# GpSimd's additions given to VectorE, one layer's constants made earlier, and another order of the last outputs: a two-layer hybrid transformer kernel

## The chip, the cores and the metric

The kernel runs on one core of one Trainium2 chip. The metric is the device time of one execution in microseconds (us). A core has five engines that run side by side and wait for one another by semaphores: TensorE (PE in the profile, with its weight loads as PEld), VectorE (DVE), ScalarE (ACT), GpSimd (POOL) and SyncE (SP), which issues the transfers between HBM and the on-chip memory SBUF. TensorE writes its products to PSUM, which is divided into banks of 128x512 floats. Each engine works through its own instructions in the order in which they stand in the program: an instruction that waits holds up everything behind it on its engine.

## The reference, cut to what matters

Two layers of a diffusion backbone over 1024 latent tokens and 256 context tokens, model width 1024, all in float32:

```python
for l in range(2):
    h  = rms_norm(x, g1[l]) * (1 + sc1) + sh1          # sh, sc, gt: silu(c) @ w_mod[l] + b_mod[l]
    mix = concat(window_attention(rope(q), rope(k), v), # 8 heads on 2 KV heads, +-128 tokens and the context
                 fourier_mix(u, w_fourier[l]),          # 2-D DFT per group of channels, then a linear map
                 gla(gq, gk, gv, gr, gz))               # gated linear attention in chunks of 64, both directions
    x  = x + gt1 * (mix @ w_out[l])
    h2 = rms_norm(x, g2[l]) * (1 + sc2) + sh2
    gate, up = split(h2 @ w_ffn_in[l])                  # 1024 -> 2 x 2816
    x  = x + gt2 * ((silu(gate) * up) @ w_ffn_out[l])   # 2816 -> 1024
    # layer 0 does the same for the context tokens
```

## The kernel before, in words

Activations lie with features on the 128 partitions: a feature block of 128 by 512 tokens is one tile, and the 1024 latent tokens are two halves, c = 0 and c = 1. A float32 product is made of three passes (`mm3`, lines 168 to 170): each operand is split by `split` into a rounded high part (a cast on ACT, line 163) and the rest, value minus high part (a subtraction on DVE, line 164), and TensorE adds high times high, high times rest and rest times high. So each weight tile and each activation tile costs one ACT cast and one DVE subtraction before TensorE can use it. In the profile `wh`, `wl` and `HC` are split weights, `F`, `H` and `HC` split activations, `raw` and `XC` weights as loaded, and `f`, `mm`, `t`, `g` PSUM banks (four `f`, two of each other).

A layer has a mixed stage (projections, attention, Fourier mixing, gated linear attention, output projection, woven together), then the FFN, then the down projection. Layer 0 runs to about 1705 us of the trace, layer 1 from there to the end.

- **The mixed stage.** `project` makes queries and keys with their rotary factors (line 597 the multiplication by the sine, on POOL). `attend` and `gla` run beside it; in `gla` line 876 adds two masked 128x256 halves and line 906 multiplies the normalised output by a gate tile `sr` that has just been loaded, both on POOL. `layer_consts(l)` at the start of each layer loads the gate weights, the Fourier weights and constants of that layer, and makes `a12` from them by eight small matmuls (line 229; two rows of four in the order).
- **The FFN.** `ffn_plain` does the first few of the 22 blocks f of 128 hidden channels in the usual way. `ffn_seven` does the rest, both token halves at once, with seven products in place of eight for a two-by-two block product (gate and up against feature halves; the Winograd form of Strassen's scheme). For that it needs sums of activations, made once (`combos1` and `combos2`, lines 1156 and 1164: the differences and the running sum on POOL, the sums with "+" in their names on DVE), and for each f five sums of 128x512 weight tiles (`weights`, line 1222, on POOL, tile `c`), each then split by ACT and DVE. Weights are made three products ahead of their use. The four results of an f are put together by ACT copies and DVE additions (lines 1268 to 1286), and the last read of a PSUM bank frees it for a later product. In layer 0 the modulation vectors of layer 1 are made on the side: two 128x1024 tiles of `wmodT` for each f are loaded into `raw` and reduced on DVE (line 328).
- **The down projection** (`ffn_lat`, `down_mm`). For each half c it goes over all 22 f, and for each f over the 8 output blocks m, adding into 8 PSUM banks: m = 0 to 3 are `f` banks, 4 and 5 are `mm`, 6 and 7 are `t`. `done(m)` (line 1370) adds the finished block to the residual on DVE, which frees its bank, and stores it. After c = 1 of layer 0 comes layer 1: `layer_consts(1)`, and the first projection of its mixed stage (lines 516 to 518: high by high, high by rest, and `wl` by high).

What sets the order: the program emits work as interleaved streams with planned costs, and a scheduler of the Tile framework places each instruction in its engine's order. TensorE has 12,699 rows in that order; in the mixed stages about a thousand of them stand elsewhere after the change.

Of the kernel before, what the change touches and what calls it, by code (L numbers as in the profile page):

```python
# [16 lines left out]
KT = 8  # L17
# [3 lines left out]
FT = 22  # L21
# [3 lines left out]
FS = ("F", 20)  # L25
LAG = 3
REST = (32, 20)
NA = 6
# [16 lines left out]
class Prog:  # L45
# [374 lines left out]
    def layer(self, l):  # L420
        nc, tc = self.nc, self.tc
        need = l < DEPTH - 1
        self.layer_consts(l)
        XA = self.XA = self.t(self.bp, [128, 8, 512], F32, "XA", 1)
# [160 lines left out]
    def qk(self, l, s, nm, j, ps, t0, n, rope):  # L585
# [9 lines left out]
        if rope is not None:  # L595
            nc.vector.stream_shuffle(sq, raw, mask=[(i + 16) % 32 for i in range(32)])
            nc.gpsimd.tensor_tensor(sq, sq, rope[:, 1, :], ALU.mult)
            nc.vector.tensor_tensor(raw, raw, rope[:, 0, :], ALU.mult)
            nc.vector.tensor_tensor(raw, raw, sq, ALU.add)
# [122 lines left out]
    def gla(self, l, s, need):  # L722
# [34 lines left out]
        for j in range(2):  # L757
# [99 lines left out]
            for c in range(nq):  # L857
# [3 lines left out]
                for hh in range(2):  # L861
                    qd, en, st, _ = heads[hh]
                    tps = []
                    for d in range(2):
                        tp = self.g_ps(cw)
                        rows = slice(d * 64, d * 64 + 64)
                        for b in range(cw // 128):
                            bs = slice(c * cw + b * 128, c * cw + (b + 1) * 128)
                            nc.tensor.matmul(tp[:, b * 128:(b + 1) * 128], en[rows, bs], qd[rows, bs], start=True, stop=True)
                        tps.append(tp)  # L870
                    at = tmp("e")
                    for z in range(0, cw, 256):
                        for d in range(2):
                            nc.vector.copy_predicated(
                                self.abuf[d], self.glam[d][:].rearrange("p a b -> p (a b)"), tps[d][:, z:z + 256])
                        nc.gpsimd.tensor_tensor(at[:, z:z + 256], self.abuf[0], self.abuf[1], ALU.add)
                    ats.append(at)
                    yield 2.0
# [26 lines left out]
                nc.sync.dma_start(sr, self.dram[s, "sr"][j, :, cs])  # L905
                nc.gpsimd.tensor_tensor(ob, ob, sr, ALU.mult)
                nc.sync.dma_start(self.dram[s, "mix"][:, 6 + j, cs], ob)
# [243 lines left out]
    def combo(self, name, pool, tag, parts):  # L1151
        self.B[name] = self.half(pool, tag)
        for k in range(4):
            a, b, op = parts(k)
            t = self.t(self.tp, [128, 512], F32, "nx", 3)[:]
            (self.nc.vector if "+" in name else self.nc.gpsimd).tensor_tensor(t, a, b, op)
            self.split(t, *self.B[name](k))
            yield 1

    def combos2(self):  # L1160
        r, x = self.raw0, self.raw1
        yield from self.combo("7+", self.fp, FS, lambda k: (r(k + 4), x(k + 4), ALU.add))
        for k in range(4):
            self.nc.gpsimd.tensor_tensor(r(k), r(k), x(k), ALU.add)
            yield 1
# [33 lines left out]
    def ffn_seven(self, l, fs, fps):  # L1199
# [7 lines left out]
        def weights(i):  # L1207
# [12 lines left out]
            if isinstance(pair, tuple):  # L1220
                src = self.t(self.tp, [128, 512], F32, "c1", 2)[:]
                nc.gpsimd.tensor_tensor(src, *pair)  # L1222
            else:
# [73 lines left out]

    def down_mm(self, ps, w, g, f, ms):
        for m in ms:
            s = slice(m * 128, (m + 1) * 128)  # L1300
            self.mm3(ps[m], w[0][:, s], w[1][:, s], g[:, 0, :], g[:, 1, :], f == 0, f == FT - 1)

    def ffn_lat(self, l):
# [5 lines left out]
        with tc.tile_pool(name=f"ffn{l}", bufs=2, reuse_waits="tile") as self.fp, \  # L1309
# [13 lines left out]
            for f in self.ffn_seven(l, list(range(f0, FT)), fps):  # L1323
                if mod is not None:
                    if f == f0 + 4:
                        nrc = self.t(self.tp, [128, NC], F32, "nrc", 1)
                        nc.vector.tensor_copy(nrc[:], self.norm_stats(self.streamed(self.xcsrc, 0, NC), NC, True))
                    for _ in range(2):
                        next(mod, None)
# [12 lines left out]
            for c in range(2):  # L1342
# [33 lines left out]
                else:  # L1376
                    for m in range(KT):
                        done(m)
# [111 lines left out]
```

## Time and profile before

| | |
|---|---|
| three runs, median (lowest to highest) | 3032.04 us (3027.81 to 3037.07) |
| the profiled execution: its own time / span of the trace | 3032.16 us / 3030.4 us |
| mean granted TensorE clock over the span | 0.959 of full speed |
| PE busy | 2810.1 us (93%) |
| DVE busy | 1925.5 us (64%) |
| ACT busy | 1362.1 us (45%) |
| POOL busy | 365.6 us (12%) |

The span runs from the first to the last record of the trace; about 1.8 us of the execution lie outside it. An engine's busy time counts its instructions' own duration, not its waits. The granted clock of TensorE has two levels, 1.2 and 2.4 GHz, written as 0.5 and 1.0.

### The profile page before, as it was taken

What the parts mean: (1) busy time and instruction counts of PE and PEld (TensorE: products, weight loads), DVE (VectorE), ACT (ScalarE), POOL (GpSimd) and SP (SyncE); (2) the same over time, 40 slices, a digit from 0 to 9 for tenths busy, and PEclk for the clock granted to TensorE, in tenths of its full rate; (3) what the DMA queues carried; (4) which work ended last, traced back from release to release, by engine and by line L of the source; (5) the groups of instructions that cost most, each with busy time, mean ns of one, the idle gap of its engine ahead of it and who ended that gap; (6) DMA issues with size and microseconds to landing.
All of it is one profiled execution on the core that took longest, in us unless ns stands there. A gap on an engine that the chain in (4) does not pass through costs nothing. (4 is left out here: it accounts for less than half of the span.)

```text
span 3030.4 us, 38144 instructions
## 1 busy us (share of the span) xinstructions
PE 2810.1 (93%) x14042; PEld 2248.4 (74%) x14042; DVE 1925.5 (64%) x3041; ACT 1362.1 (45%) x2476; POOL 365.6 (12%) x266
## 2 busy tenths in 40 slices
PE   6999997979989889999999898996898999999999
PEld 3577676868888677887877776664676887888887
DVE  4266677787675877777547468685675567555332
ACT  3356565565554533333324356554445454333321
POOL 0000100000000434332000000010100014331000
PEclk9999997989999999999999999996899999999999
DMA  7754452434555244444746534334244332224542
GB/s 250 257 159 132 127 156 72 144 94 138 178 185 180 84 165 134 141 135 145 257 160 214 190 112 141 114 94 139 86 127 152 125 126 94 84 84 136 201 157 94
DMA packets 198042, 436.45 MB, mean 144 GB/s; under 512 B 23712, under 2 KB 59296, under 8 KB 196832
## 3 DMA queue, kind: packets, MB, share of 16 engines
q1 hardware_dynamic: 197856, 434.03, 44.1%
q8 instruction: 110, 1.80, 0.2%
q14 instruction: 76, 0.62, 0.1%
HBM read 361.85 MB, written 69.48 MB: 142 GB/s over the span
## 5 line engine op out<-in xcount | busy, mean ns | idle before, releaser
L164 DVE TENSOR_TENSOR wl<-raw,wh 128x1024 fp32r<-128x1024 f32 (+1 forms) x310 | 377.4, 1220 | 365.2 <-ACT wh L163 345.3
L163 ACT CAST wh<-raw 128x1024 fp32r<-128x1024 f32 (+2 forms) x319 | 325.7, 1025 | 528.2 <-PE mm L169 194.6
L168 PE MATMUL mm<-H,wh 128*128 128x512 f32 x716 | 290.4, 408 | 4.1 <-ACT H L163 3.7
L170 PE MATMUL mm<-H,wl 128*128 128x512 f32 x728 | 290.7, 401 | 0.0
L169 PE MATMUL mm<-H,wh 128*128 128x512 f32 x716 | 287.9, 404 | 0.8 <-DVE H L164 0.8
L168 PE MATMUL mm<-F,wh 128*128 128x512 f32 x536 | 210.4, 392 | 6.6 <-ACT F L163 3.9
L169 PE MATMUL mm<-F,wh 128*128 128x512 f32 x536 | 210.6, 393 | 0.7 <-DVE F L164 0.7
L170 PE MATMUL mm<-F,wl 128*128 128x512 f32 x524 | 205.7, 393 | 0.5 <-DVE wl L164 0.5
L168 PE MATMUL f<-F,wh 128*128 128x512 f32 x444 | 174.0, 392 | 13.8 <-ACT GC L1268 12.3
L170 PE MATMUL f<-F,wl 128*128 128x512 f32 x456 | 177.5, 390 | 0.4 <-DVE wl L164 0.4
L169 PE MATMUL f<-F,wh 128*128 128x512 f32 x444 | 173.4, 391 | 0.0
L168 PEld LDWEIGHTS mm<-H,wh 128*128 128x128 f32 x716 | 136.3, 191 | 37.1 <-issue 5.8
L168 PE MATMUL mm<-HC,wh 128*128 128x256 f32 x544 | 160.0, 295 | 3.2 <-ACT HC L163 1.8
L170 PEld LDWEIGHTS mm<-H,wl 128*128 128x128 f32 x728 | 138.4, 190 | 30.2 <-issue 2.7
L169 PEld LDWEIGHTS mm<-H,wh 128*128 128x128 f32 x716 | 136.6, 191 | 29.8 <-issue 1.9
L169 PE MATMUL mm<-HC,wh 128*128 128x256 f32 x544 | 157.2, 290 | 0.6 <-DVE HC L411 0.3
L170 PE MATMUL mm<-HC,wl 128*128 128x256 f32 x544 | 155.4, 287 | 0.8 <-DVE wl L164 0.8
L328 DVE CUSTOM_DVE_ANT_0 na<-raw,GC 128x1024 bf16<-128x1024 f32 x64 | 90.0, 1406 | 88.9 <-DMA raw<-wmodT 84.9
L674 ACT ACTIVATE P<-S,nm 128x640 f32<-128x640 f32 (+2 forms) x144 | 104.6, 732 | 71.4 <-DVE nm L670 70.7
L168 PEld LDWEIGHTS mm<-F,wh 128*128 128x128 f32 x536 | 101.1, 189 | 30.5 <-ACT F L163 5.5
L668 DVE TENSOR_REDUCE mx<-S 128x2 f32<-128x1280 f32 (+2 forms) x68 | 95.6, 1406 | 40.9 <-PE S L663 40.4
L696 PE MATMUL t<-ident,P 128*128 128x128 f32 x640 | 110.5, 289 | 11.6 <-DVE pt L701 4.3
(592 smaller groups left out, 6989.7 us busy)
## 6 DMA issues: line engine op xcount, KB each, us to landing
raw<-wff SPq DMA_DIRECT2D x228, 512.0 KB, 3.8
raw<-wmodT SPq DMA_DIRECT2D x64, 512.0 KB, 4.1
raw<-wfm SPq DMA_DIRECT2D x52, 512.0 KB, 4.0
nx<-gd SPq DMA_DIRECT2D x88, 256.0 KB, 3.8
raw<-wout SPq DMA_DIRECT2D x40, 512.0 KB, 3.7
XC<-wff SPq DMA_DIRECT2D x34, 512.0 KB, 3.8
pt<-wmod SPq DMA_DIRECT2D x64, 256.0 KB, 4.5
qld<-q_l SPq DMA_DIRECT2D x64, 256.0 KB, 4.2
```

What stands on the lines that cost most here:

```text
L163: self.nc.scalar.copy(hi, raw)
L164: (eng or self.nc.vector).tensor_tensor(lo, raw, hi.bitcast(F32), ALU.subtract)
L168: mm(ps, wh, xh, start=start, stop=False, skip_group_check=skip)
L169: mm(ps, wh, xl, start=False, stop=False, skip_group_check=skip)
L170: mm(ps, wl, xh, start=False, stop=stop, skip_group_check=skip)
L328: self.nc.vector.tensor_tensor_reduce(out=junk[:], in0=raw, in1=cs[s][:], op0=ALU.mult, op1=ALU.add, scale=1.0, scalar=0.0, accum_out=self ...
L668: nc.vector.tensor_reduce(mx[:, :nh], st[:, c0:c0 + nh * n].rearrange("p (a n) -> p a n", n=n), axis=AX.X, op=ALU.max)
L674: nc.scalar.activation(P[:, :n], st[:, c0 + z * n:c0 + (z + 1) * n], ACTF.Exp, bias=nm[:, hh:hh + 1], accum_out=sums[:, hh:hh + 1])
L696: nc.tensor.transpose(tp[:, hh * 128:(hh + 1) * 128], P[:, c:c + 128], self.ident[:])
```

## The change

All 260 additions, subtractions and multiplications of GpSimd go to VectorE: lines 597 (20 of them), 876 (36), 906 (10), 1156 (16), 1164 (8) and 1222 (170: five sums for each of 34 f). GpSimd keeps only the fills of tiles with constants. `layer_consts(1)` is called inside layer 0's FFN, after the block f = f0 + 8, and no longer at the start of layer 1; its three loads stand in SP's order ahead of that. In the down projection the last f goes over the output blocks in the order 6, 7, 4, 5, 0, 1, 2, 3, and `done` follows the same order except in c = 0 of layer 0.

```diff
+LASTM = (6, 7, 4, 5, 0, 1, 2, 3)
...
     def layer(self, l):
         nc, tc = self.nc, self.tc
         need = l < DEPTH - 1
-        self.layer_consts(l)
+        if l == 0:
+            self.layer_consts(l)
...
             nc.vector.stream_shuffle(sq, raw, mask=[(i + 16) % 32 for i in range(32)])
-            nc.gpsimd.tensor_tensor(sq, sq, rope[:, 1, :], ALU.mult)
+            nc.vector.tensor_tensor(sq, sq, rope[:, 1, :], ALU.mult)
             nc.vector.tensor_tensor(raw, raw, rope[:, 0, :], ALU.mult)
...
-                        nc.gpsimd.tensor_tensor(at[:, z:z + 256], self.abuf[0], self.abuf[1], ALU.add)
+                        nc.vector.tensor_tensor(at[:, z:z + 256], self.abuf[0], self.abuf[1], ALU.add)
...
                 nc.sync.dma_start(sr, self.dram[s, "sr"][j, :, cs])
-                nc.gpsimd.tensor_tensor(ob, ob, sr, ALU.mult)
+                nc.vector.tensor_tensor(ob, ob, sr, ALU.mult)
...
             t = self.t(self.tp, [128, 512], F32, "nx", 3)[:]
-            (self.nc.vector if "+" in name else self.nc.gpsimd).tensor_tensor(t, a, b, op)
+            self.nc.vector.tensor_tensor(t, a, b, op)
             self.split(t, *self.B[name](k))
...
         for k in range(4):
-            self.nc.gpsimd.tensor_tensor(r(k), r(k), x(k), ALU.add)
+            self.nc.vector.tensor_tensor(r(k), r(k), x(k), ALU.add)
...
                 src = self.t(self.tp, [128, 512], F32, "c1", 2)[:]
-                nc.gpsimd.tensor_tensor(src, *pair)
+                nc.vector.tensor_tensor(src, *pair)
...
     def down_mm(self, ps, w, g, f, ms):
+        if f == FT - 1:
+            ms = LASTM
         for m in ms:
...
                         nc.vector.tensor_copy(nrc[:], self.norm_stats(self.streamed(self.xcsrc, 0, NC), NC, True))
+                    if f == f0 + 8:
+                        self.layer_consts(l + 1)
...
                 else:
-                    for m in range(KT):
+                    for m in LASTM:
                         done(m)
```

In the rows of the order below, the changed kernel's line numbers are one higher than before from line 26 and two higher from line 424: line 163 is 164 there, 1268 is 1270, 1270 is 1272, 1370 is 1376, 516 to 518 are 518 to 520.

**The first place** is the head of `ffn_seven` in layer 0, where the first block's products run while the sums of activations are still being made. On ACT before, `GC<-f` is the copy that frees the bank of the first product, and the `H` casts around it take tiles `nx` that POOL makes on line 1156:

```order
L163 CAST HC_1698_9631<-c1_1697_9629 128x512
L163 CAST H_1662_9498<-nx_1666_9502 128x512
L576 ACTIVATE nx_1659_9485<-nx_1659_9485 128x512
L163 CAST wh_1704_9657<-c1_1703_9655 128x512
L163 CAST wl_1706_9682<-c1_1705_9680 128x512
L163 CAST H_1662_9498<-nx_1667_9506 128x512
L163 CAST H_1663_9499<-nx_1669_9537 128x512
L1268 COPY GC_1671_9546<-f_1681_9567 128x512
L163 CAST wh_1716_9740<-XC_1696_9626 128x512
```

On ACT now, at the same copy:

```order
L164 CAST wl_1693_9603<-raw_1673_9548 128x512
L578 ACTIVATE nx_1659_9485<-nx_1659_9485 128x512
L1270 COPY GC_1671_9546<-f_1681_9567 128x512
L164 CAST H_1662_9498<-nx_1666_9502 128x512
L164 CAST H_1662_9498<-nx_1667_9506 128x512
L164 CAST H_1663_9499<-nx_1669_9537 128x512
```

The copy stands ahead of the `H` casts, and no cast of a weight sum (`HC_1698`, `wh_1704`, `wl_1706`) stands ahead of it any more.

On DVE before, at the addition of line 1270 that reads the second product's bank (`GC<-GC,f`), with the last sums of activations around it:

```order
L164 TENSOR_TENSOR wl_1706_9682<-c1_1705_9680,wl_1706_9682 128x512
L1156 TENSOR_TENSOR nx_1690_9578<-XA_60_382,F_1486_8446 128x512
L164 TENSOR_TENSOR H_1665_9501<-nx_1670_9541,H_1663_9499 128x512
L1156 TENSOR_TENSOR nx_1691_9582<-XA_60_382,F_1486_8446 128x512
L164 TENSOR_TENSOR F_1688_9576<-nx_1690_9578,F_1686_9574 128x512
L1156 TENSOR_TENSOR nx_1692_9586<-XA_60_382,F_1487_8447 128x512
L164 TENSOR_TENSOR F_1688_9576<-nx_1691_9582,F_1686_9574 128x512
L1156 TENSOR_TENSOR nx_1694_9606<-XA_60_382,F_1487_8447 128x512
L164 TENSOR_TENSOR F_1689_9577<-nx_1692_9586,F_1687_9575 128x512
L1270 TENSOR_TENSOR GC_1671_9546<-GC_1671_9546,f_1682_9568 128x512
```

On DVE now, around the same addition (line 1272; line 1224 makes the sums of weights, line 1166 the running sum of activations):

```order
L1158 TENSOR_TENSOR nx_1694_9606<-XA_60_382,F_1487_8447 128x512
L1166 TENSOR_TENSOR XA_60_382<-XA_60_382,F_1484_8444 128x512
L1272 TENSOR_TENSOR GC_1671_9546<-GC_1671_9546,f_1682_9568 128x512
L165 TENSOR_TENSOR F_1689_9577<-nx_1694_9606,F_1687_9575 128x512
L1224 TENSOR_TENSOR c1_1697_9629<-XC_1696_9626 128x512
L1166 TENSOR_TENSOR XA_60_382<-XA_60_382,F_1485_8445 128x512 x2
L165 TENSOR_TENSOR HC_1698_9631<-c1_1697_9629,HC_1698_9631 128x512
L165 TENSOR_TENSOR F_1701_9638<-XA_60_382,F_1699_9636 128x512
L1274 TENSOR_TENSOR HC_1672_9547<-f_1683_9569,GC_1671_9546 128x512
L1224 TENSOR_TENSOR c1_1703_9655<-raw_1695_9625 128x512
L165 TENSOR_TENSOR F_1701_9638<-XA_60_382,F_1699_9636 128x512
L165 TENSOR_TENSOR wh_1704_9657<-c1_1703_9655,wh_1704_9657 128x512
```

From the subtraction `wl_1657<-raw_1655,wh_1656` (128x1024, line 164) to this addition there stand 32 rows of DVE before (the subtraction counted, the addition not), and 41 now; the weight sums `c1_1697` (the fourth product's `HC_1698`) and `c1_1703` now stand behind the addition, where before they and their subtractions were done ahead of it.

**The second place** is the end of layer 0. On DVE before, the eight `done` of the second half, in the order f, f, f, f, mm, mm, t, t, and then the rests of the first weights of layer 1:

```order
L344 TENSOR_SCALAR a_1l_14347<-a_1l_14347 128x8
L1370 SCALAR_TENSOR_TENSOR F_12543<-f_13465,mod_0l,F_12543 128x512
...
L1370 SCALAR_TENSOR_TENSOR F_12544<-f_13468,mod_0l,F_12544 128x512
L1370 SCALAR_TENSOR_TENSOR F_12545<-mm_13469,mod_0l,F_12545 128x512
L1370 SCALAR_TENSOR_TENSOR F_12545<-mm_13470,mod_0l,F_12545 128x512
L1370 SCALAR_TENSOR_TENSOR F_12546<-t_13471,mod_0l,F_12546 128x512
L1370 SCALAR_TENSOR_TENSOR F_12546<-t_13535,mod_0l,F_12546 128x512
L164 TENSOR_TENSOR wl_14431<-raw_14428,wh_14430 128x832
```

On DVE now:

```order
L345 TENSOR_SCALAR a_1l_14362<-a_1l_14362 128x8
L1376 SCALAR_TENSOR_TENSOR F_12561<-t_13486,mod_0l,F_12561 128x512
L1376 SCALAR_TENSOR_TENSOR F_12561<-t_13550,mod_0l,F_12561 128x512
L1376 SCALAR_TENSOR_TENSOR F_12560<-mm_13484,mod_0l,F_12560 128x512
L1376 SCALAR_TENSOR_TENSOR F_12560<-mm_13485,mod_0l,F_12560 128x512
L1376 SCALAR_TENSOR_TENSOR F_12558<-f_13480,mod_0l,F_12558 128x512
...
L1376 SCALAR_TENSOR_TENSOR F_12559<-f_13483,mod_0l,F_12559 128x512
L165 TENSOR_TENSOR wl_14431<-raw_14428,wh_14430 128x832
```

On PE before, from the last matmul of the down projection on:

```order
L170 MATMUL t_2317_13535<-F_2460_14307,wl_2458_14302 128x512
L229 MATMUL mm_2471_14377<-nx_2469_14373 128x128 x4
L516 MATMUL t_2483_14422<-wh_2490_14430,HC_2326_13553 128x416
L517 MATMUL t_2483_14422<-wh_2490_14430,HC_2328_13555 128x416
L516 MATMUL t_2484_14423<-wh_2490_14430,HC_2326_13553 128x416
L517 MATMUL t_2484_14423<-wh_2490_14430,HC_2328_13555 128x416
L516 MATMUL mm_2485_14424<-wh_2490_14430,H_2318_13545 128x416
L517 MATMUL mm_2485_14424<-wh_2490_14430,H_2322_13549 128x416
L516 MATMUL mm_2486_14425<-wh_2490_14430,H_2318_13545 128x416
L518 MATMUL t_2483_14422<-wl_2491_14431,HC_2326_13553 128x416
```

On PE now:

```order
L171 MATMUL f_2318_13483<-F_2465_14322,wl_2463_14317 128x512
L518 MATMUL t_2483_14422<-wh_2490_14430,HC_2331_13568 128x416
L519 MATMUL t_2483_14422<-wh_2490_14430,HC_2333_13570 128x416
L518 MATMUL t_2484_14423<-wh_2490_14430,HC_2331_13568 128x416
L519 MATMUL t_2484_14423<-wh_2490_14430,HC_2333_13570 128x416
L518 MATMUL mm_2485_14424<-wh_2490_14430,H_2323_13560 128x416
L519 MATMUL mm_2485_14424<-wh_2490_14430,H_2327_13564 128x416
L518 MATMUL mm_2486_14425<-wh_2490_14430,H_2323_13560 128x416
L519 MATMUL mm_2486_14425<-wh_2490_14430,H_2327_13564 128x416
L518 MATMUL g_2487_14426<-wh_2490_14430,H_2323_13560 128x416
L519 MATMUL g_2487_14426<-wh_2490_14430,H_2327_13564 128x416
L518 MATMUL g_2488_14427<-wh_2490_14430,H_2323_13560 128x416
```

The small matmuls of `layer_consts(1)` are gone from here (they stand between two products of the FFN now), and 12 matmuls that need only `wh` come ahead of the first one that needs `wl`, where there were 7.

## Rows read from the trace of the kernel before

**Rows 1.** The page: busy time of each engine, share, instructions.
```profile
PE 2810.1 (93%) x14042; PEld 2248.4 (74%) x14042; DVE 1925.5 (64%) x3041; ACT 1362.1 (45%) x2476; POOL 365.6 (12%) x266
```
**Rows 2.** Windows: length, busy us and instructions by engine, PEclk granted, DMA share, GB/s.
```profile
1022.00:1066.00 44.00, 28.46 (x110) 22.71 (x109) 42.07 (x40) 21.45 (x40) 31.79 (x19) 0.82 0.19 60
1066.00:1425.00 359.00, 349.55 (x1507) 285.30 (x1506) 281.81 (x367) 121.92 (x215) 132.81 (x92) 0.98 0.43 142
...
2499.00:2569.00 70.00, 65.37 (x285) 52.81 (x283) 48.31 (x63) 33.63 (x60) 31.74 (x21) 1.00 0.26 87
...
1062.60:1067.00 4.40, 4.40 (x11) 3.43 (x12) 4.40 (x8) 3.93 (x10) 0.00 (x0) 0.50 0.34 94
```
**Rows 3.** Timeline of PE, layer 0's FFN head: start, duration, idle before and releaser.
```profile
1053.24 0.80 PE L168 MATMUL f<-F,wh 128*128 128x512 f32 x1 [10.88 <-ACT GC L1268]
...
1062.54 0.80 PE L168 MATMUL f<-H,wl 128*128 128x512 f32 x1 [4.66 <-DVE GC L1270]
```
**Rows 4.** Timeline of ACT there.
```profile
1052.08 0.62 ACT L163 CAST H<-nx 128x512 fp32r<-128x512 f32 x1 [1.05 <-POOL nx L1156]
1052.60 0.58 ACT L1268 COPY GC<-f 128x512 f32<-128x512 f32 x1
```
**Rows 5.** Timeline of POOL there (19 such rows from 1022.03 to 1057.7).
```profile
1041.15 1.73 POOL L1222 TENSOR_TENSOR c<-raw 128x512 f32<-128x512 f32 x1
```
**Rows 6.** Timeline of DVE there.
```profile
1022.05 1.22 DVE L164 TENSOR_TENSOR wl<-raw,wh 128x1024 fp32r<-128x1024 f32 x1
...
1029.77 1.77 DVE L164 TENSOR_TENSOR wh<-c,wh 128x512 fp32r<-128x512 f32 x1
...
1061.21 0.68 DVE L164 TENSOR_TENSOR F<-nx,F 128x512 fp32r<-128x512 f32 x1
1061.81 0.67 DVE L1270 TENSOR_TENSOR GC<-GC,f 128x512 f32<-128x512 f32 x1
```
**Rows 7.** Lines of DVE from 1066 to 1425 (count, busy us, mean ns, idle before).
```profile
L328 DVE CUSTOM_DVE_ANT_0 na<-raw,GC 128x1024 bf16<-128x1024 f32 x39 | 59.4, 1524 | 49.1 <-DMA raw<-wmodT 45.1 <-DMA GC<-cs 3.9
L164 DVE TENSOR_TENSOR HC<-c,HC 128x512 fp32r<-128x512 f32 x36 | 31.1, 865 | 4.6 <-ACT HC L163 4.5
L164 DVE TENSOR_TENSOR wh<-c,wh 128x512 fp32r<-128x512 f32 x28 | 26.5, 946 | 7.8 <-ACT wh L163 7.3
L164 DVE TENSOR_TENSOR wl<-c,wl 128x512 fp32r<-128x512 f32 x28 | 26.2, 936 | 1.4 <-ACT wl L163 1.2
L1282 DVE TENSOR_TENSOR XA<-XA 128x512 f32<-128x512 f32 x17 | 24.2, 1421 | 2.4 <-ACT XA L1281 1.4
...
L1286 DVE TENSOR_TENSOR XA<-XA 128x512 f32<-128x512 f32 x17 | 12.1, 710 | 0.1
```
**Rows 8.** Timelines of PE, DVE and ACT from layer 0 to layer 1.
```profile
1705.71 2.07 PE L229 MATMUL mm<-nx 128*128 128x128 f32 x8 [5.72 <-DVE F L1370]
...
1709.42 0.35 PE L518 MATMUL t<-wl,HC 128*128 128x416 f32 x1
...
1702.28 2.72 DVE L1370 SCALAR_TENSOR_TENSOR F<-f,mod_0l,F 128x512 f32<-128x512 f32 x4
...
1706.23 1.40 DVE L1370 SCALAR_TENSOR_TENSOR F<-t,mod_0l,F 128x512 f32<-128x512 f32 x2
1707.55 1.95 DVE L164 TENSOR_TENSOR wl<-raw,wh 128x832 fp32r<-128x832 f32 x2
...
1702.96 0.88 ACT L163 CAST wh<-raw 128x832 fp32r<-128x832 f32 x1 [9.56 <-DMA raw<-wtm]
```
**Rows 9.** Waits of PE, 2058 to 2077: us in total, times, longest.
```profile
PE g L811 <- DVE c L803: 15.2, 1, 15.2
```
**Rows 10.** Timeline of DVE inside that wait.
```profile
2066.57 1.75 DVE L594 SCALAR_TENSOR_TENSOR XA<-XA,nqkg 128x512 f32<-128x512 f32 x1
```
**Rows 11.** Timelines of DVE and POOL in layer 0's mixed stage.
```profile
322.31 0.48 DVE L903 SCALAR_TENSOR_TENSOR nacc<-nacc,nglg,nx 128x256 f32<-128x256 f32 x1
...
325.80 0.74 POOL L906 TENSOR_TENSOR nacc<-nacc,nx 128x256 f32<-128x256 f32 x1 [11.18 <-DMA nx<-sr_c]
```

## The prediction

> **What bounds the kernel now.** I read the page's busy times first, then windows of the span, then what TensorE waits for in the windows where it is idle. TensorE is busy 93% of the span and no other engine more than 64% [rows 1]: the kernel is bound by TensorE, and time can only come out of its idle stretches, some 220 us of 3030.4, and out of the half-clock stretches behind them. The reader should see in the windows where POOL's work lies and whether TensorE waits there. From 1066 to 1425, the steady FFN of layer 0, POOL is busy 133 us, but TensorE 349.6 of 359 [rows 2]; only 9.4 us can be had. In the head of that FFN, 1022 to 1066, TensorE is busy 28.5 of 44 us and DVE 42.1 of 44 [rows 2]. This is the one stretch where DVE is full and TensorE waits for it, so I looked there most closely.
>
> TensorE's two waits there are 10.88 us for the ACT copy of line 1268 and 4.66 us for the DVE addition of line 1270 [rows 3]. The copy itself takes 0.58 us and starts the moment the cast ahead of it is through; that cast waited for POOL's line 1156 [rows 4]. So the copy is late because it stands in ACT's order behind casts of sums that POOL makes one after another at 1.7 us each, 19 of them without a pause worth naming [rows 5]. The addition is late because DVE, with 32 instructions from 1022.05 to 1061.81, took 1.24 us for each. An undisturbed one of that size takes 0.68 and the next starts 0.60 after it; those beside a POOL instruction take up to 1.77 [rows 6]. POOL slows DVE down, so what is handed back to DVE is not simply added to it.
>
> A page of the Trainium skill, "SBUF — State Buffer", section "Who interferes with whom", says that a DVE instruction with two SBUF inputs contends with a GpSimd instruction that reads SBUF, and that one of the two is blocked for the other's whole instruction. The 1.77 beside 0.68 agrees with that.
>
> **The change part by part.** *All additions to DVE, the work.* 222 of the 260 are 128x512: 222 x 0.68 [rows 6] = 151 us, and the 38 of 256 columns at most the 0.48 of line 903's 128x256 form [rows 11], 18 us; DVE gets some 169 us more. Against this its excess beside POOL goes. In the steady FFN, 1066 to 1425, I take four groups: the rests `HC`, `wh`, `wl` at 865, 946 and 936 ns against 680 (36 x 0.185 + 28 x 0.266 + 28 x 0.256 = 21 us), and line 1282 at 1421 against its twin 1286 at 710 (17 x 0.71 = 12 us) [rows 7]. That is 33 us, and line 328 and the smaller groups have some more; POOL's 92 instructions there would cost 92 x 0.68 = 63 us on DVE. So DVE's busy time of 281.8 us grows by at most 30, to 312 of 359 [rows 2]. It has room: TensorE stays the bound.
>
> *The head of layer 0's FFN.* In the new order 41 DVE instructions stand ahead of the addition that freed the bank last, in place of 32. At 0.60 each, with 0.53 more for the wide first one, that is 25.1 us: from 1022.05 to 1047.2, where it was 1061.8 [rows 6]. That is the lower bound if DVE never waits for ACT's casts; they interleave one to one, so I add 3 us and take 1050. The ACT copy now stands ahead of the `H` casts and waits for no sum: the 10.88 us go, down to what the addition then sets. TensorE's fourth product starts 12 matmuls (2.8 us) after 1042.36 (1053.24 less 10.88) at the earliest and at 1050.6 by the addition, where it was 1062.54 [rows 3]: 12 us earlier. Behind it the split weights are now made later in DVE's order: the fourth product's `HC` rest 4 rows behind the addition, the next `wh` 10 rows, the next `wl` 16 rows, thus at 1052.6, 1056.5 and 1060 against products of 2.8 us that begin at 1050.6. Each is late by up to 2 us, and half clock costs some 2 us again as it did (11 matmuls in 4.4 us at 0.5 [rows 2]). I take 12 us gained; 17.7 (both waits and the second slow stretch) is the most, and 5 the least, if DVE spends 10 us on waits for casts.
>
> *The rest of layer 0's FFN.* 9.4 us of idle [rows 2], partly short waits for ACT and DVE. I take 4, bounds 0 and 9.
>
> *The head of layer 1's FFN*, 2499 to 2569: 4.6 us of idle [rows 2], POOL as full as in layer 0, but DVE only 48 of 70. I take 3, bounds 0 and 4.6.
>
> *Fourier constants and the order of outputs.* Between the layers TensorE stands from 1699.99 to 1705.71 until line 1370 frees the `mm` bank that line 229 wants, runs eight small matmuls (2.07 us), and reaches the first `wl` matmul at 1709.42 with 7 `wh` matmuls done. Now the first two `done` free the `t` banks by about 1703.7 and the next two `mm` by 1705, ACT has cast `wh` at 1703.84, and 12 `wh` matmuls can run. But `wl` stands behind all eight `done` on DVE, as before, and is there at about 1708.5 [rows 8]. So TensorE comes to the first `wl` matmul 0.8 us earlier, with 5 more matmuls of 0.19 us behind it: 2 us, not the whole wait of 5.72. The constants' matmuls take half of 2.07, about 1 us, at full clock in the FFN. Their three loads stand far ahead of their use on SP and land under the 19 us of matmuls that an f takes; if that cover were missing, a late load costs some 3 us, as the gate tile's does [rows 11]. Net 1 us; the bounds are a loss of 1 and a gain of 5.7. At the end of the kernel the last output block still follows the last matmul, whichever it is: nothing, bounds 0.7 either way (one instruction of DVE).
>
> *The mixed stages.* The largest wait of layer 1, 15.2 us for DVE's line 803 [rows 9], has on its chain the multiplication of line 594 at 1.75 us beside POOL's line 906 [rows 10]; another one on it is slowed likewise by line 597. Without POOL they give back 2 x 1.07 us, and lines 906 and 597, now in DVE's order themselves, take up to 2 x 0.6 of that: 1 us. Over all mixed stages DVE's excess and the added instructions about balance, while each chain from DVE to POOL and back loses a pair of waits; I take 5 us gained with that 1 in it. Here about a thousand rows of TensorE stand elsewhere, and no row of before prices that: I take 15 us either way, the size of the largest single wait there. Line 906 brings a new wait: the loaded gate tile. It came 3 us after line 903 ended (322.79 to 325.80 [rows 11]), and on DVE all behind it would wait, weight rests among them. Ten of them at 3 us would be 30, nothing the least; POOL's group as a whole was ahead of TensorE's need, so I count one, 3 us, inside the 5.
>
> **The sum** against the profiled execution: 12 + 4 + 3 + 1 + 5 = 25 us off 3032.16 gives 3007 us. Its own time and the median of 3032.04 are the same to 0.1 us, so no correction is needed. A measurement of this kernel can tell about 0.3%, 9 us, from no change.
>
> **The rivals.** *DVE becomes the bound in the steady FFN (slower).* An f takes TensorE 19.3 us (84 matmuls of 0.23: 1507 took 349.6 us). DVE has 15.2 us of work for each of the 18.6 in this window, and waits 45.1 / 18.6 = 2.4 us for `wmodT` loads [rows 2, 7], during which POOL could still add, while a DVE addition now stands behind that wait. If the excess stays (slow for another reason than POOL), DVE needs 15.2 + 5 x 0.68 + 2.4 = 21.0 us, 1.7 over: 19 f x 1.7 = 32 us lost, less the 9 won elsewhere (3 + 1 + 5): about 3055. The point that decides is 19.3 us of work and wait. For it: DVE is in order, and its waits come every f. Against it: line 1286 at 710 beside 1282 at 1421 is the same operation on the same size [rows 7], so the excess is POOL's. A page of the Trainium skill, "Perfetto Trace Analysis", section "Optimizing Scalar/DVE Operations", advises offloading some work from a saturated DVE to GpSimd, with the reservation that the two share a port; read by its first half the head of the FFN should lose what the change puts on DVE, 19 x 0.68 = 13 us, and by the second not. Rows 6 speak for the second.
>
> *The mixed stages lose what the FFN gains (slower or nothing).* One more wait like that of 15.2 us in each layer, with TensorE at half clock for some microseconds behind it, costs about 18 us each: 25 - 36 = -11, about 3043. The gated attention and the line 906 wait are the places; it decides from 25 us lost on.
>
> *The head only shifts (no change).* If ACT's casts and DVE's rests hand the wait on within the head (each sum needs add, cast, rest, two engine changes), 5 us come of it, and with 1 at the boundary and the rest nothing: 3026.
>
> **How the numbers follow.** The forecast has 0.60, its own range 2995 to 3021 (the head at 5 to 17.7, the other stages at half or one and a half of their terms). More than that, with the mixed stages at their good bound: 0.07, about 2985. Only a shift: 0.14, 3026. Mixed stages lose: 0.12, 3043. DVE bound: 0.07, 3055. The range 2988 to 3034 leaves out half of the good end, the DVE case and most of the mixed case, 2 in 10. Faster by over 0.3% (under 3023): 0.60 + 0.07 + a third of the shift = 0.72; within: the rest of the shift and a share of the mixed losses, 0.14; slower: 0.14.
>
> **What the profile after would show.** No DVE instruction of 128x512 with two inputs over 0.8 us. TensorE's waits in the head down from 15.5 to under 5 us, with the addition of line 1272 some 12 to 15 us earlier after the wide `wl`. In the steady FFN, DVE at 15 to 17 us of work per f and TensorE busy as before. At the boundary a first `wl` matmul about 1.5 us earlier, still released by DVE. Wrong would be: waits of TensorE for `c` weights (lines 164 and 165) in each f; or new waits over 5 us in the mixed stages.

## The result, and the profile after

The changed kernel takes 2994.64 us (median of four runs, 2991.04 to 2999.45), the kernel before, run beside it, 3033.78 (3027.81 to 3037.07): a ratio of 0.9874 with a 95% interval of 0.9853 to 0.9896, 39 us less where 25 were forecast. The profiled execution took 2991.04 us with a span of 2989.3, 41.1 us under the span before.

The page of the changed kernel, busy time of each engine, as in rows 1:
```profile
PE 2799.3 (94%) x14042; PEld 2245.9 (75%) x14042; DVE 1955.0 (65%) x3301; ACT 1364.6 (46%) x2476; POOL 1.3 (0%) x6
```
DVE took over 260 instructions, 168 us by the sum of their durations, and its busy time, which counts an overlap of two instructions once, grew by 29.5: the instructions that it did before as well take 122 us less in sum. Of its two-input instructions of 128x512 (lines with TENSOR_TENSOR), 105 of 1234 took more than 0.8 us before; of 1456 now, none does, as the prediction's signs had it.

Where the 41.1 us went can be read by the starts of the same instructions in both traces (line numbers of before):

| from, to | before | after | difference |
|---|---|---|---|
| start to the third line 1194 (mixed stage of layer 0, output projection) | 1026.09 | 1028.49 | +2.4 |
| to the second copy of line 1268 (head of layer 0's FFN) | 45.97 | 31.78 | -14.2 |
| to the 20th copy of line 1268 (rest of that FFN) | 366.06 | 350.63 | -15.4 |
| to the last line 337 (down projection of layer 0) | 263.65 | 262.62 | -1.0 |
| to the 32nd line 1079 (boundary, mixed stage of layer 1) | 702.86 | 696.14 | -6.7 |
| to the 24th copy of line 1268 (head of layer 1's FFN) | 175.88 | 169.75 | -6.1 |
| to the end | 449.9 | 449.8 | 0 |

The three stretches of the FFN come out alike in another execution of the changed kernel (e10 below: 30.3, 350.5 and 169.7); the stretch of layer 1's mixed stage does not (702.4 there, 696.1 here), so most of its -6.7 is what one execution may differ from another. The +2.4 of layer 0's mixed stage is as uncertain; the experiments below settle both.

Windows of the changed kernel (columns as in rows 2): the head and the rest of layer 0's FFN, and the head of layer 1's.
```profile
1022.00:1066.00 44.00, 41.00 (x170) 33.43 (x169) 40.91 (x67) 28.28 (x51) 0.00 (x0) 0.92 0.17 54
1066.00:1405.00 339.00, 338.25 (x1495) 279.63 (x1494) 280.26 (x462) 124.23 (x212) 0.00 (x0) 1.00 0.48 159
...
2460.00:2540.00 80.00, 80.00 (x355) 66.26 (x354) 65.55 (x103) 38.83 (x67) 0.00 (x0) 1.00 0.32 105
```
DVE does 67 instructions in the 44 us in which it did 40 [rows 2], and is busy no longer. TensorE, idle 15.5 us there before, is idle 3.0; in the 339 us behind, 0.75.

Timelines of ACT, DVE and PE in that head, as in rows 3, 4 and 6:
```profile
1040.46 0.59 ACT L1270 COPY GC<-f 128x512 f32<-128x512 f32 x1 [1.59 <-PE f L171]
...
1025.55 1.22 DVE L165 TENSOR_TENSOR wl<-raw,wh 128x1024 fp32r<-128x1024 f32 x1
...
1050.77 0.67 DVE L1272 TENSOR_TENSOR GC<-GC,f 128x512 f32<-128x512 f32 x1
...
1051.59 0.77 PE L169 MATMUL f<-H,wl 128*128 128x512 f32 x1 [3.00 <-ACT F L164]
```
The copy now waits for TensorE's product and for nothing else: the wait of 10.88 us is gone. From the wide `wl` to the addition it is 25.2 us, where it was 39.8 and the rows of the order gave 25.1.

Lines of DVE from 1070 to 1405, as in rows 7:
```profile
L329 DVE CUSTOM_DVE_ANT_0 na<-raw,GC 128x1024 bf16<-128x1024 f32 x40 | 48.9, 1222 | 16.2 <-DMA raw<-wmodT 15.4 <-DMA GC<-cs 0.7
...
L165 DVE TENSOR_TENSOR HC<-c,HC 128x512 fp32r<-128x512 f32 x35 | 23.9, 683 | 0.0
L165 DVE TENSOR_TENSOR wh<-c,wh 128x512 fp32r<-128x512 f32 x28 | 19.2, 685 | 0.3 <-ACT wh L164 0.2
```
The means of 865 and 946 ns are 683 and 685 now, that of the modulation's reduction 1222 for 1524. DVE is busy 280 us of 339 (83%), where it was busy 282 of 359 (78%), with POOL's additions in it now (92 of them in the window before).

Timelines at the end of layer 0, as in rows 8:
```profile
1675.09 0.65 PE L518 MATMUL t<-wh,HC 128*128 128x416 f32 x1 [2.63 <-ACT wh L164]
...
1680.37 0.46 PE L520 MATMUL t<-wl,HC 128*128 128x416 f32 x1 [0.28 <-DVE wl L165]
...
1674.03 1.40 DVE L1376 SCALAR_TENSOR_TENSOR F<-t,mod_0l,F 128x512 f32<-128x512 f32 x2
...
1676.66 2.71 DVE L1376 SCALAR_TENSOR_TENSOR F<-f,mod_0l,F 128x512 f32<-128x512 f32 x4
1679.30 1.01 DVE L165 TENSOR_TENSOR wl<-raw,wh 128x832 fp32r<-128x832 f32 x1
```
From the end of the down projection (1672.46) to the first `wl` matmul it is 7.9 us where it was 9.4, with 12 matmuls done and not 7; `wl` still stands behind the eight `done`.

### The profile page after: what moved, and what is told of

Its sections match the earlier page's. It is cut to its first block, busy times and chain, and to the rows that moved or that the text cites. A ratio compares the mean times of both kernels' runs of the same rounds, so it can differ in the third digit from the quotient of the medians.

```text
span 2989.3 us, 37860 instructions
## 1 busy us (share of the span) xinstructions
PE 2799.3 (94%) x14042; PEld 2245.9 (75%) x14042; DVE 1955.0 (65%) x3301; ACT 1364.6 (46%) x2476; POOL 1.3 (0%) x6
## 4 chain that ended last, share of the span: by engine, by line
PE 71%; DVE 11%; DMA 8%; ACT 6%; issue 3%; SPq 1%; ACTq 0%; DVEq 0%
PE mm L169 11%; PE mm L170 11%; PE mm L171 11%; PE f L171 5%; PE f L169 5%; PE f L170 5%; DMA raw<-wff 3%; PE t L711 2%; PE t L698 2%; PE t L170 2%; PE t L169 2%; PE t L171 2%; DVE wl L165 2%; ACT wh L164 1%; DMA nx<-gd 1%
## 5 line engine op out<-in xcount | busy, mean ns | idle before, releaser
L170 PEld LDWEIGHTS mm<-H,wh 128*128 128x128 f32 x716 | 135.9, 190 | 29.5 <-DVE H L165 2.5
L169 PEld LDWEIGHTS mm<-F,wh 128*128 128x128 f32 x536 | 101.4, 189 | 27.3 <-ACT F L164 4.5
L170 PEld LDWEIGHTS mm<-F,wh 128*128 128x128 f32 x536 | 101.5, 189 | 22.9 <-DVE F L165 1.5
```

The source lines that it names most:

```text
L169: mm(ps, wh, xh, start=start, stop=False, skip_group_check=skip)
L170: mm(ps, wh, xl, start=False, stop=False, skip_group_check=skip)
```

## The experiments

My theory after the result: the FFN's additions carry the whole gain, since POOL's additions held up DVE's instructions (and the casts and copies behind them). The rivals: the other two edits, or the new order of the mixed stages, carry a good part; or the gain in the FFN is one of shorter chains and of the order on ACT, and POOL's mere work costs nothing. All ratios are to the kernel before on the same chip.

| run | additions on DVE | other edits | us | ratio (95%) |
|---|---|---|---|---|
| e1_adds_only | all | no | 2989.9 | 0.9873 (0.9857 to 0.9889) |
| e2_no_adds | none | yes | 3028.43 | 1.0002 (0.9992 to 1.0012) |
| e3_ffn_adds | FFN's 194 | no | 2988.85 | 0.987 (0.9852 to 0.9888) |
| e4_mixed_adds | mixed stages' 66 | no | 3028.43 | 1.0006 (0.9995 to 1.0017) |
| e5_weight_sums | line 1222 | no | 2995.34 | 0.99 (0.9885 to 0.9915) |
| e6_act_sums | lines 1156, 1164 | no | 3014.41 | 0.9963 (0.995 to 0.9975) |
| e7_beside_adds | all, and POOL adds too | yes | 3089.91 | 1.0211 (1.0192 to 1.0229) |
| e8_beside_fills | all, and POOL fills | yes | 2999.0 | 0.991 (0.9895 to 0.9925) |
| e9_ffn_adds_rest | FFN's 194 | yes | 2986.36 | 0.9855 (0.9834 to 0.9876) |
| e10_after_again | all | yes | 2993.67 | 0.9881 (0.986 to 0.9902) |
| e11_mixed_layer1 | FFN's, mixed of layer 1 | yes | 2987.82 | 0.9868 (0.9853 to 0.9882) |
| e12_mixed_layer0 | FFN's, mixed of layer 0 | yes | 2996.18 | 0.9889 (0.9873 to 0.9906) |

**Which edit.** The first four, the edits taken alone or left out:

```diff
 # e1, to before: the six lines of the change with nc.gpsimd, nothing else
 # e2, to after: the same six lines back
 # e3, to before
+            self.nc.vector.tensor_tensor(t, a, b, op)
+            self.nc.vector.tensor_tensor(r(k), r(k), x(k), ALU.add)
+                nc.vector.tensor_tensor(src, *pair)
 # e4, to before
+            nc.vector.tensor_tensor(sq, sq, rope[:, 1, :], ALU.mult)
+                        nc.vector.tensor_tensor(at[:, z:z + 256], self.abuf[0], self.abuf[1], ALU.add)
+                nc.vector.tensor_tensor(ob, ob, sr, ALU.mult)
```

> The kernel before with all 260 additions on VectorE, and neither of the other two edits. Theory (the additions are nearly all of the gain): 2994.6 plus the 1 to 2 us that the boundary between the layers gave, thus 2994 to 2999, and TensorE's waits in the head of layer 0's FFN as short as in the changed kernel (3 us). Rival (the output order and the earlier constants carry a good part): 3005 to 3025.

> The changed kernel with all 260 additions back on GpSimd: only the constants of layer 1 made earlier and the other order of the last outputs. Theory: 3028 to 3036, no difference that can be told, with the wait between the layers (5.7 us before) shorter by some 2 us. Rival (these two edits carry a good part): 3005 to 3022.

> The kernel before with only the FFN's additions on VectorE (lines 1156, 1164, 1222). Theory (GpSimd beside VectorE costs in the FFN): 36 us less than before, thus about 2997, since the trace after was 30 us faster over layer 0's FFN and 6 us over the head of layer 1's. Rival (the reordering of the mixed stages gives a good part): 3005 to 3020.

> The kernel before with only the mixed stages' additions on VectorE (lines 597, 876, 906). Theory: the mixed stages were 2.5 us slower in layer 0 and 5 to 6 us faster in layer 1 in the trace after, so 3027 to 3034, no difference that can be told. Rival (the forecast's 5 us with its bounds of 15): 3015 if the chains from VectorE to GpSimd and back were on the path, 3045 if the new waits in VectorE's order are.

All four came as the theory had it, measured by ratios (this chip's kernel before took 3025, so the times expected lie some 7 us too high). The FFN's additions alone give the whole gain; the constants and the output order nothing that can be told in the total, though in e2's trace the wait between the layers is 2.1 us for 5.7, as expected. The mixed stages' additions give nothing that can be told either.

**Which sums.** Only the weight sums, and only the activation sums, on DVE (one and two of e3's lines):

> The kernel before with only the weight sums (line 1222, 170 of the 194 additions of the FFN) on VectorE; the activation sums (lines 1156, 1164) stay on GpSimd. Theory (two parts: the head's first wait hangs on the activation sums, the later waits of layer 0's FFN and VectorE's excess on the weight sums): the steady part's 13 us and some of the heads, thus 3000 to 3015 on the scale of a before of 3032, a ratio of 0.990 to 0.995. Rival (the steady part was never held by GpSimd): 0.997 to 1.001.

> The kernel before with only the activation sums (lines 1156 and 1164, 24 additions) on VectorE; the weight sums stay on GpSimd. Theory: the heads of the two FFNs, 14 and 6 us, less what the weight sums beside them still cost, so a ratio of 0.993 to 0.997, and the waits around 1097, 1127 and 1193 still there. Rival (the head's gain needs both, as each holds VectorE alone): 0.998 to 1.001.

Both ratios lie in the ranges expected (e5's at the very edge of its own), but one part of e5's theory failed. Waits of PE from 1015 to 1400, e5_weight_sums:
```profile
PE f L168 <- DVE GC L1270: 4.3, 1, 4.3
PE f L170 <- DVE HC L164: 3.6, 1, 3.6
PE f L168 <- ACT GC L1268: 1.2, 1, 1.2
PE f L168 <- ACT HC L163: 1.2, 1, 1.2
```
and e6_act_sums:
```profile
PE f L168 <- ACT HC L163: 4.7, 1, 4.7
PE f L168 <- DVE XA L1270: 2.9, 2, 2.1
PE mm L168 <- ACT XA L1268: 2.5, 1, 2.5
```
With the weight sums on DVE the wait of 10.88 us for the copy is 1.2: the theory's point that this wait hangs on the activation sums failed. The wait of 4.66 in the head remains (4.3) and one of 3.6 for `HC` is new there; of the later FFN's waits one of 1.2 is left. With the activation sums alone the head's two long waits are gone and the later ones remain, the first of them longer (4.7, where it was 2.0). The two ratios, -1.0% and -0.37%, add to e3's -1.3%, but stretch by stretch the parts do not add (us, the stretches of the table above):

| run | head of layer 0's FFN | rest of it | head of layer 1's FFN |
|---|---|---|---|
| before | 45.97 | 366.06 | 175.88 |
| e5, weight sums | 39.61 | 352.28 | 169.75 |
| e6, activation sums | 33.51 | 370.31 | 170.34 |
| e3, both | 30.26 | 349.53 | 169.75 |

In both heads each part alone gives some of the same microseconds; in the rest of layer 0's FFN the activation sums alone lose 4 us, and with the weight sums beside them gain 3. The totals add up without the parts doing so.

**Port or chain.** Do POOL's reads hold up DVE's instructions (the "port" of the expectation below), or does the gain come from shorter chains and from ACT's order? In e7 POOL does each of the FFN's sums once more, into a tile nobody reads; in e8 it adds one element and fills that tile three times. The order of PE, DVE and ACT is that of the changed kernel.

```diff
+    def beside(self, a, b):
+        self.nc.gpsimd.tensor_tensor(self.padr[:], a[:, 0:504], b[:, 0:504], ALU.add)          # e7
+        self.nc.gpsimd.tensor_tensor(self.padr[:, 0:1], a[:, 0:1], b[:, 0:1], ALU.add)         # e8
+        for _ in range(3):                                                                     # e8
+            self.nc.gpsimd.memset(self.padr[:], 0.0)                                           # e8
...
                 nc.vector.tensor_tensor(src, *pair)
+                self.beside(pair[0], pair[1])
```

> The changed kernel, with GpSimd doing each of the FFN's 194 additions once more into a tile that nothing reads (504 of the 512 columns). No instruction of TensorE, VectorE or ScalarE moves and none waits for these results. Theory (GpSimd's reads hold up VectorE's instructions with two inputs): VectorE's 512-column instructions beside them go from 0.68 up to 1.75 us, the head of layer 0's FFN loses most of its 14 us again and the steady FFN some, so 10 to 40 us over the changed kernel, a ratio to before of 0.991 to 1.001. Rival (the gain was the shorter chains and ACT's order, not the port): the same time as the changed kernel, 0.986 to 0.989.

> The changed kernel, with GpSimd as long at work as in the run before, but writing only: for each of the 194 additions one element is added (to start at the same point) and a 504-column tile is filled three times, 0.5 us each. Theory (the reads contend): VectorE's instructions stay at 0.68 us and the time is that of the changed kernel, a ratio to before of 0.986 to 0.989. Rival (any work of GpSimd slows VectorE): 0.991 to 1.001, like the run before.

e7 lost 3.4% against the changed kernel, about 100 us: the theory's direction, and more than twice its size. Timelines of DVE and POOL in e7:
```profile
1207.74 0.68 DVE L1294 TENSOR_TENSOR XA<-t,XA 128x512 f32<-128x512 f32 x1
...
1209.42 1.75 DVE L1295 TENSOR_TENSOR XA<-XA 128x512 f32<-128x512 f32 x1
1211.10 1.77 DVE L1230 TENSOR_TENSOR c<-raw 128x512 f32<-128x512 f32 x1
1212.78 1.75 DVE L165 TENSOR_TENSOR HC<-c,HC 128x512 fp32r<-128x512 f32 x1
...
1216.65 0.68 DVE L165 TENSOR_TENSOR wh<-c,wh 128x512 fp32r<-128x512 f32 x1
...
1207.44 1.51 POOL L1165 TENSOR_TENSOR padr<-raw 128x504 f32<-128x504 f32 x1 [6.14 <-DMA raw<-wff]
1209.03 3.28 POOL L1165 TENSOR_TENSOR padr<-raw,XC 128x504 f32<-128x504 f32 x2
1212.39 1.60 POOL L1165 TENSOR_TENSOR padr<-XC,raw 128x504 f32<-128x504 f32 x1
```
and the window of its FFN:
```profile
1066.00:1405.00 339.00, 303.78 (x1256) 243.53 (x1257) 313.20 (x400) 110.77 (x193) 141.30 (x88) 0.94 0.39 132
```
From 1209 to 1215 the two take turns, one instruction each, 1.68 us a pair; the DVE instruction of 1207.74, one of whose inputs lies in PSUM, keeps its 0.68 beside POOL. Over the whole run 169 of DVE's 1456 two-input instructions of 128x512 take more than 0.8 us (none in the changed kernel), and no instruction of DVE, ACT or TensorE waits over 0.1 us for POOL. DVE is busy 313 of 339 us and waits for loads besides; it has become the bound, as the first rival of the prediction described it (22.1 us for each f from the second copy of line 1268 to the 20th, where the rival had 21.0 and the changed kernel takes 19.5), and my 10 to 40 us had counted delay but not that bound.

The same window and two lines of DVE (from 1070) in e8, and a wait for POOL that it adds, from DVE's timeline:
```profile
1066.00:1405.00 339.00, 336.66 (x1486) 278.21 (x1485) 280.88 (x463) 123.23 (x210) 192.47 (x379) 1.00 0.47 157
...
L329 DVE CUSTOM_DVE_ANT_0 na<-raw,GC 128x1024 bf16<-128x1024 f32 x40 | 48.9, 1223 | 17.6 <-DMA raw<-wmodT 15.0 <-DMA nx<-xc 2.3
...
L165 DVE TENSOR_TENSOR HC<-c,HC 128x512 fp32r<-128x512 f32 x35 | 23.9, 683 | 0.0
...
1061.44 0.69 DVE L165 TENSOR_TENSOR F<-XA,F 128x512 fp32r<-128x512 f32 x1 [4.28 <-POOL padr L1165]
```
POOL is busy longer than in e7 (192 us) and DVE's instructions keep 683 ns; none of the 1456 takes more than 0.8 us. Filling does not disturb, reading does. The total, 0.991, is still outside the 0.986 to 0.989 that I expected, and on the edge of the rival's range: it is by DVE's durations, not by the total, that e8 decides. The trace shows one cause of the excess, a DVE instruction that has to wait until POOL's one-element addition has read the tile that it overwrites (4.28 us, passed on to TensorE as 4.7; a copy of ACT waits 4.57 us for POOL at the same place). It is a wait of the experiment's own making. A later wait of TensorE is 2.0 us (0.4 in the changed kernel), and together the head and the rest of layer 0's FFN are 6.0 us longer than in the changed kernel (388.4 and 382.4); this is about half of the 11 us, and the rest stays open.

So POOL's reads slow DVE, and that by itself can cost far more than the change gave. How much of the gain comes from DVE's faster instructions, and how much from shorter chains and ACT's new order, these runs do not separate.

**The mixed stages.**

```diff
 # e9, to after: lines 597, 876, 906 (599, 878, 908) with nc.gpsimd; e10 is the changed kernel
 # e11, to after, these three lines
-            nc.vector.tensor_tensor(
+            (nc.vector if l else nc.gpsimd).tensor_tensor(
 # e12, to after, these three lines
+            (nc.gpsimd if l else nc.vector).tensor_tensor(
```

> The changed kernel with the mixed stages' additions (lines 597, 876, 906) back on GpSimd: the FFN's additions on VectorE, the constants of layer 1 made earlier, the last outputs in the new order. Theory (the mixed stages' additions bring nothing on VectorE, or cost a little): the changed kernel's time or up to 5 us less, a ratio to before of 0.985 to 0.988. Rival (the forecast's 5 us gained in the mixed stages): 2 to 8 us over the changed kernel run beside it, 0.988 to 0.990.

> The changed kernel once more on the same chip as the run before, to be compared with it: 0.986 to 0.989 of before by every theory.

> The changed kernel with the mixed stages' additions on GpSimd in layer 0 and on VectorE in layer 1. Theory (they lose in layer 0, where a wait of 10.5 us became 14.0 and one of 6.6 became 8.2, and gain or lose little in layer 1, where 15.2 became 12.2 and 4.65 became 7.5): layer 0 as in the run without them, so a ratio to before of 0.984 to 0.987 and 3 to 8 us less than the run below. Rival (no difference by layer): the same as the run below.

> The changed kernel with the mixed stages' additions on VectorE in layer 0 and on GpSimd in layer 1. Theory: the waits of 14.0 and 8.2 us in layer 0 are there, the one of 15.2 in layer 1 too; a ratio to before of 0.987 to 0.990. Rival (no difference by layer): the same as the run above.

e9 was 7.3 us under e10, and e11 8.4 us under e12 (differences of medians on one chip; the intervals of the ratios overlap in both pairs). For e11 against e12, 3 to 8 us were expected. The stretches of the profiled executions tell more (seven with layer 0's additions on GpSimd: before, e2, e3, e5, e6, e9 and e11; for layer 1 with e12 in place of e11; the other five: e1, e4, after, e10 and e12 or e11):

| stretch | seven with its additions on GpSimd | five with them on VectorE |
|---|---|---|
| start to the third line 1194, layer 0's additions | 1020.1 to 1026.1, mean 1022.3 | 1025.8 to 1030.8, mean 1028.0 |
| last line 337 to the 32nd line 1079, layer 1's additions | 700.0 to 706.0, mean 703.0 | 696.1 to 702.4, mean 699.9 |

So on VectorE they lose some 6 us in layer 0 and gain some 3 in layer 1. Waits of PE over the whole of e11_mixed_layer1:
```profile
PE g L813 <- DVE c L805: 28.3, 6, 12.2
PE g L813 <- issue: 14.3, 7, 6.6
PE g L813 <- ACT nacc L391: 10.5, 1, 10.5
```
and of e12_mixed_layer0:
```profile
PE g L813 <- DVE c L805: 28.1, 6, 15.2
PE g L813 <- issue: 14.7, 5, 8.2
PE g L813 <- ACT nacc L391: 14.0, 1, 14.0
```
In layer 1 the wait of 15.2 us becomes 12.2, but the total for line 805 stays at 28: another wait took over what the first gave back. In layer 0 the wait for ACT's line 391 goes from 10.5 to 14.0, and the longest `issue` from 6.6 to 8.2. The loss lies in layer 0, as the theory had it, but not as idle time: up to the third line 1194 TensorE is idle 97.7 us in e11 and in e12. It is at half clock for 85.3 us of that stretch in e11 and for 112.6 in e12 (85.3 to 99.0 in the seven executions, 109.2 to 116.1 in the five), and most of the difference lies from 600 to 700 us, in e11 and then in e12:
```profile
600.00:700.00 100.00, 79.70 (x568) 69.36 (x569) 77.78 (x136) 54.79 (x104) 5.06 (x4) 0.90 0.32 103
600.00:700.00 100.00, 78.75 (x519) 70.11 (x521) 76.81 (x133) 54.48 (x103) 0.00 (x0) 0.78 0.28 90
```
Which waits in the new order keep the clock down for longer is not shown. e9, without the mixed stages' additions, is the fastest kernel here by its median, 42 us under before; how far it leads the changed kernel is not settled by these runs (some 3 us by the means of the table).

## Why the prediction was right, point by point

- **The bound.** Right: TensorE remained it, and the gain came out of its idle stretches. That POOL slows DVE, so that the additions do not simply add up, was the step on which the sign rested; e7 and e8 show it directly. The page "SBUF — State Buffer" of the Trainium skill, section "Who interferes with whom", has the same rule for a VectorE instruction with two SBUF inputs, and says that a GpSimd instruction that only writes does not contend with it; e8's 683 ns agree.
- **The head of layer 0's FFN:** 12 us forecast, 14.2 measured. The addition came 25.2 us after the wide `wl` (25.1 as the lower bound, 28 taken): DVE did not once wait for ACT's casts in between, so the 3 us added for them were not needed.
- **The rest of that FFN:** 4 us forecast, 15.4 measured, above the bound of 9. This is the term that was mis-sized. I had taken TensorE's idle time of 9.4 us from the window and halved it. Nearly all of it went (0.75 is left), two waits of 1.0 and 1.2 us at the end of the window and behind it went too, and so did the time at half clock behind three of the waits, which a busy TensorE does not show as idle. Windows of the kernel before around three of those waits:
```profile
1096.00:1101.00 5.00, 3.76 (x9) 2.74 (x10) 4.05 (x4) 2.38 (x4) 3.75 (x4) 0.67 0.17 62
1127.00:1132.00 5.00, 4.61 (x12) 3.16 (x12) 5.00 (x6) 1.87 (x4) 3.27 (x2) 0.66 0.28 91
1192.00:1197.00 5.00, 3.94 (x10) 3.15 (x11) 4.33 (x8) 0.51 (x1) 0.20 (x1) 0.66 0.79 282
```
  A granted clock of 0.67 over 5 us is a third of it lost, 1.7 us, three times; it is 1.00 there now. I had counted this loss in the head and not here. e5 shows that the weight sums did most of it: on DVE alone they take 13.8 us off this stretch, the activation sums alone none.
- **The head of layer 1's FFN:** 3 forecast, up to 6.1 measured over a wider stretch; in the window shown TensorE has no idle time left.
- **Constants and output order:** net 1 forecast; in the trace 1.5 us and 5 matmuls of 0.19 us at the boundary, 2.5 against the 2 forecast, with `wl` the next to be late as written. e2 finds no difference in the total.
- **The mixed stages:** 5 us gained forecast, none measured in the total (e4: +0.06%, with an interval of -0.05 to +0.17%), and by the stretches some 6 us lost in layer 0 and 3 gained in layer 1. The direction of this term failed. The chain of line 803 did get shorter, by 3 us where 1 was worked out, but handed the time on: the wait behind it went from 4.65 to 7.5 us, a new wait over 5 us in a mixed stage, which the prediction had named as a sign of being wrong. The loss in layer 0 is time at half clock, which the sum did not count there. The gate tile's wait, priced at 3 us, was 0.5 us, once.
- **The rivals.** DVE as the bound did not happen, because the excess went; e7 shows that it would have with the excess in place. The mixed stages lost far less than the rival's 36 us.

So the forecast held with two errors of opposite sign in it: 11 us too little in the steady FFN, 5 us or more too much in the mixed stages. That they partly cancel is luck. The 2994.64 us lie in the stated range of 2988 to 3034, but just under the 2995 to 3021 that the prediction gave its own sum.

## What to carry to other kernels

Before giving elementwise work to GpSimd to relieve VectorE, or taking it back, compare VectorE's durations beside GpSimd's with those alone: here the 260 additions on GpSimd saved VectorE 29.5 us of busy time, for 168 us of work, and cost the kernel 1.3%. When a short wait of TensorE may go, count the half clock behind it as well as the idle time, and look at both when a new order costs time: in layer 0's mixed stage the idle time stayed the same. Where many chains share TensorE, as in the mixed stages, one shorter chain promises little: ask which wait comes up behind it.

## What the runs showed of the hardware that was not expected

GpSimd is held up too, and for longer than one instruction. In e8 its addition of a single element took 5.93 us while VectorE had a row of instructions with two SBUF inputs back to back, and the next such addition 2.40; timelines of POOL and DVE:
```profile
1045.27 5.93 POOL L1165 TENSOR_TENSOR padr<-XA,F 128x1 f32<-128x1 f32 x1 [13.42 <-DVE XA L1173]
...
1053.01 2.40 POOL L1165 TENSOR_TENSOR padr<-XA,F 128x1 f32<-128x1 f32 x1
...
1059.22 0.19 POOL L1165 TENSOR_TENSOR padr<-XA,F 128x1 f32<-128x1 f32 x1
...
1051.07 0.67 DVE L1281 TENSOR_TENSOR GC<-GC,f 128x512 f32<-128x512 f32 x1
...
1055.28 0.67 DVE L1283 TENSOR_TENSOR HC<-f,GC 128x512 f32<-128x512 f32 x1
```
The same instruction takes 0.19 us where VectorE has stopped (it waited from 1057.2 to 1061.4). Both long ones end just as VectorE comes to an instruction with one input in PSUM (1051.20 beside 1051.07, 1055.41 beside 1055.28). So an engine that looks slow in a trace may be one that waits inside its instruction.
